# Sixteen attention weight tiles split early and kept in DRAM, and three smaller edits of an attention stage

## The chip, the cores and the metric

The kernel runs on one core of one Trainium2 chip. A core has five engines with queues of their own: TensorE (PE, matmuls), VectorE (DVE), ScalarE (ACT), GpSimd (POOL) and SyncE (SP, which issues the DMAs here). The metric is the device time of one execution, in microseconds, as the median of several; beside it stands one execution taken by the hardware profiler, and all rows below are of that one.

## The reference, cut to what matters

Two layers work on 512 tokens of width 1024, in float32. Each layer is a mixer and an MLP, and both end in `x = LN(alpha*x + (1+gate)*f(x*(1+scale)+shift))`, where shift, scale and gate are products of one conditioning vector with large "modulation" matrices. The mixer of the first layer is a gated linear attention, the one of the second is softmax attention over 64-token chunks, and the change is about the second:

```
q, k, v = split(u @ w_in + b_in, 3)              # 16 heads of 64
s = q*k / 8 + rel_bias[head, clipped distance]   # own chunk and the 8 before it
o = softmax(masked s) @ v
out = o @ w_out
mlp: square(relu(u @ w1)) @ w2                   # width 4096
```

A row of the softmax sums to one, so `softmax(s) @ (v + b)` is `softmax(s) @ v + b`.

## The kernel before, in words

Activations lie with the 1024 features on partitions, as eight tiles of 128 x 512. Every weight comes in units of 512 KB (128 x 1024, the eight 128 x 128 blocks that make one output tile). To get float32 accuracy from the faster float32r matmul, a unit is split on chip: `hi` is the unit rounded to float32r (a cast on ScalarE) and `lo = raw - hi` (a subtraction on VectorE, `lo_of`). A product is then three matmuls, hi*hi, hi*lo and lo*hi (`mm3`), so that one output tile (`mtile`) is 24 matmuls of 128 x 512. The activations are split in the same manner.

The list `plan` holds all units of the program in the order of their use. `emit_unit` takes the next one, issues its load on SyncE into a `raw` buffer (a pool of five) and its cast and subtraction, and puts the pair into the queue `ready_w`; `next_w` hands out one and `fill` keeps some units ahead. Pairs lie in the pool `wp` (four each of `whi` and `wlo`) or, for a few, in the pool `act` (26 tiles of 128 x 1024, `fhi` and `flo`, shared with all activations `ar` and `af`). Kinds of units: "w" as told, "p" with the subtraction on GpSimd, "e", "f" and "F" in `act` tiles, "a" a modulation unit: a load, and one VectorE operation that multiplies it with the conditioning vector and sums. The 48 modulation units that remain lie between the units of the first MLP, one after each of its 48 middle weights (`add_mlp`).

VectorE, ScalarE, GpSimd and TensorE run in the order of the program text, which the class `InOrder` fixes; every instruction recorded through it has line 46 of the kernel before (47 of the one after), so rows are told apart by the names of their tiles. The order of SyncE's queue is left to the scheduler of the framework. All engines wait for each other by semaphores, and a queue whose head waits holds back what is behind it.

Attention (`att`) begins with the value projections (`vpass`, two passes of four units) and goes on in a loop over six pairs of heads. An iteration makes one query tile and one key tile (`mtile` twice, evacuated by `evac_qk`, whose parts are `q_hi`, `q_lo`, `k_hi`, `k_lo`) and runs the softmax of two heads: `s_mm` the scores, `s_a` the evacuation with the bias and the maximum over keys, begun on VectorE and ended by an all-reduce on GpSimd (`mb`), `s_b1` the subtraction of the maximum on VectorE, `s_b2` the exponential on ScalarE, `pv` the product with the values, which also gives the sum of the row. A pair is divided by its sum in `fin1` (ScalarE: evacuation of the sum, and exp(-log) as a first reciprocal y), `fin2` (VectorE: one Newton step y(2 - sy) and the products) and `fin3` (split of the result). Six of the eight query and key pairs, p = 2 to 7, are projected in this loop; the first two come before it. The tail (`t1` to `t5`) finishes the last heads between the matmuls of the output projection `a_o`, whose first four units are kind "e".

Of the kernel before, what the change touches and what calls it, by code (L numbers as in the profile page):

```python
# [15 lines left out]
P = 128  # L16
# [39 lines left out]


@with_exitstack
def trunk(ctx, tc, xT, c, ada, cols, gk1, gk2, w_qk, w_v, w_g, w_go, a_qk, a_v, a_bv, a_tab,
          a_win, a_o, f1, f2, out):  # L60
    nc = tc.nc
    V, A, G, T = (InOrder(tc, e) for e in (nc.vector, nc.scalar, nc.gpsimd, nc.tensor))
# [4 lines left out]
    rawp = ctx.enter_context(tc.tile_pool(name="rawp", bufs=5))  # L67
    wp = ctx.enter_context(tc.tile_pool(name="wp", bufs=4))
    psp = ctx.enter_context(tc.tile_pool(name="psp", bufs=8, space=bass.MemoryType.PSUM))

    out_k = out.rearrange("(k p) s -> p k s", p=P)
    uid = [0]
# [52 lines left out]
    def ada_unit(l, t, k):  # L125
        raw = rawp.tile([P, D], F32, tag="raw", name=nm("raw"))
        nc.sync.dma_start(out=raw, in_=ada[l, t * 8 + k])
        if (l, t, k) == (0, SH1, 0):
            nc.sync.dma_start(out=col, in_=cols)
            for ll in range(2):  # L130
                for ty in (SC1, G1, SC2, G2):
                    b = C_ADA + ll * 48 + ty * 8
                    G.tensor_scalar(out=col[:, b:b + 8], in0=col[:, b:b + 8], scalar1=1.0, scalar2=None, op0=ALU.add)
            G.tensor_scalar(out=bq8, in0=col[:, C_BQ:C_BQ + 8], scalar1=0.125, scalar2=None, op0=ALU.mult)
            G.tensor_scalar(out=nbgk, in0=col[:, C_BGK:C_BGK + 4], scalar1=-1.0, scalar2=None, op0=ALU.mult)
            G.tensor_scalar(out=gn2, in0=col[:, C_GN:C_GN + 8], scalar1=-0.5, scalar2=None, op0=ALU.mult)
        if t == SC1 and l == 0:
            nc.sync.dma_start(out=xs[k], in_=xT[k * P:(k + 1) * P, :])
        i = t * 8 + k
        V.scalar_tensor_tensor(out=raw, in0=raw, scalar=1.0, in1=csil, op0=ALU.mult, op1=ALU.mult,  # L140
                               accum_out=mods[:, l, i:i + 1])
        if l == 0 and t in (SH1, SC1):
            if t == SC1:
                m2 = mods[:, 0, 0:16].rearrange("p (a b) -> p a b", b=8)[:, :, k:k + 1]
                c2 = col[:, C_ADA:C_ADA + 16].rearrange("p (a b) -> p a b", b=8)[:, :, k:k + 1]
                tt(V, m2, m2, c2, ALU.add)
        elif t == G2:
            tt(V, mods[:, l, i:i + 1], mods[:, l, i:i + 1], col[:, C_ADA + l * 48 + i:C_ADA + l * 48 + i + 1], ALU.add)
# [8 lines left out]
    state = {"pos": 0, "look": 0}  # L157
    ready_w, ready_f = [], []

    def emit_unit():  # L160
        kind, what = plan[state["pos"]]
        state["pos"] += 1
        if kind == "a":
            ada_unit(*what)
            return
        raw = rawp.tile([P, D], F32, tag="raw", name=nm("raw"))
        if state["pos"] == 3:
            for q in range(2):
                nc.sync.dma_start(out=raw[:, q * S:(q + 1) * S], in_=what[:, q * S:(q + 1) * S])
        else:  # L170
            nc.sync.dma_start(out=raw, in_=what)
        if kind in "eEfF":
            hi = act.tile([P, D], F32R, tag="act", name=nm("fhi"))
            lo = act.tile([P, D], F32R, tag="act", name=nm("flo"))
        else:
            hi = wp.tile([P, D], F32R, tag="whi", name=nm("whi"))
            lo = wp.tile([P, D], F32R, tag="wlo", name=nm("wlo"))
        if state["pos"] == 3:
            V.tensor_copy(hi[:, 0:S], raw[:, 0:S])
            later.append(lambda: A.copy(out=hi[:, S:D], in_=raw[:, S:D]))  # L180
            later.append(lambda: lo_of(V, lo, raw, hi))
            ready_w.append((hi, lo))
            return
        if kind == "s":
            for q in range(2):
                A.copy(out=hi[:, q * S:(q + 1) * S], in_=raw[:, q * S:(q + 1) * S])
        else:
            A.copy(out=hi, in_=raw)
        lo_of(G if kind in "pEF" else V, lo, raw, hi)
        (ready_f if kind in "fF" else ready_w).append((hi, lo))  # L190

    def fill(n=None):
# [28 lines left out]
    def add_out(units, fgs, adas=(), early=False, pool=0):  # L221
        adas = list(adas)
        for i, u in enumerate(units):
            plan.append(("e" if early and i < 4 else "p" if i < pool else "w", u))
            if fgs and not early and 1 < i < 6:
                plan.append(("f", fgs[i - 2]))
            if adas and i < 4:
                plan.append(("a", adas.pop(0)))
        for a in adas:
            plan.append(("a", a))  # L230
        if early:
            plan.extend(("fF"[i // 2], u) for i, u in enumerate(fgs))
# [10 lines left out]
    fg1 = lambda l: [f1[l, m] for m in range(4)]  # L243
    add_out([w_go[k] for k in range(8)], fg1(0))

    def add_mlp(l, fgs, ad):
        ad = list(ad)
        for m in range(4, 8):
            plan.append(("p" if m < 5 else "w", f1[l, m]))
        rest = [u for g in range(3) for u in [f2[l, g * 8 + m] for m in range(8)] + [f1[l, g * 8 + 8 + m] for m in range(8)]]  # L250
        add_units(rest, ad)
        add_out([f2[l, 24 + m] for m in range(8)], fgs)

    add_mlp(0, [a_qk[0], a_qk[8], a_qk[1], a_qk[9]], ada_list(0, G2) + ada_list(1, SH1, SC1, G1, SC2, SH2))
    add_units([a_v[k] for k in range(2)], kind="p")
    add_units([a_v[k] for k in range(2, 8)])
    for p in range(2, 8):
        add_units([a_qk[p], a_qk[8 + p]])
    add_out([a_o[k] for k in range(8)], fg1(1), early=True)
    add_mlp(1, [], ada_list(1, G2))  # L260

# [601 lines left out]
    def att(u):  # L863
# [37 lines left out]
        def s_a(h):  # L901
            sA, sB, b = sab[h]
            sAf = sA.rearrange("p a b -> p (a b)")
            s = [sAf[:, 0:S], sAf[:, S:S + 384], sB[:, 0, 0:256], sAf[:, S + 384:2 * S]]
            for j in range(4):
                ps = sps[h][j]
                off = max(W[j], 256) - W[j]
                nb = min(W[j], 256)
                stt(s[j][:, 0:nb], ps[:, off:off + nb], ng[:, h:h + 1], b[:, 0:nb], ALU.add, ALU.add)
                if W[j] > 256:  # L910
                    A.copy(out=s[j][:, 256:W[j]], in_=ps[:, 256:W[j]])
            mx = sB[:, 1, :]
            V.tensor_copy(mx[:, 0:P], s[0][:, 0:P])
            tt(V, mx[:, P:S], s[0][:, P:S], s[1], ALU.max)
            tt(V, mx[:, 256:S], mx[:, 256:S], s[2], ALU.max)
            tt(V, mx[:, 384:S], mx[:, 384:S], s[3], ALU.max)
            mb = ab_.tile([P, S], F32, tag="mb", name=nm("mb"))
            G.partition_all_reduce(mb, mx, P, bass_isa.ReduceOp.max)
            st[h] = (s, sAf)
            mbs[h] = mb  # L920
# [40 lines left out]
        def fin2(p):  # L961
            s, y, pa, pb = fin[p]
            tt(V, s, s, y, ALU.mult)
            V.tensor_scalar(out=s, in0=s, scalar1=-1.0, scalar2=2.0, op0=ALU.mult, op1=ALU.add)
            tt(V, y, y, s, ALU.mult)
            tt(V, s[0:64, :], pa[0:64, :], y[0:64, :], ALU.mult)
            tt(V, s[64:128, :], pb[64:128, :], y[64:128, :], ALU.mult)

        def fin3(p):
            s = fin[p][0]  # L970
            r = act_r()
            A.copy(out=r[:, 0, :], in_=s)
            lo_of(V, r[:, 1, :], s, r[:, 0, :])
            o.append(r)

        bv = act_f()
        nc.sync.dma_start(out=bv.rearrange("p a b -> p (a b)"), in_=a_bv.to_broadcast([P, D]))

        def vpass(n, hooks):
            pvb = [bank() for _ in range(4)]  # L980
            for j in range(4):
                w = next_w()
                for kk in range(2):
                    k = 2 * j + kk
                    for i in range(4):
                        mm3(pvb[i], uk(u, k, i * P, (i + 1) * P), wk(w, kk, S), k == 0, k == KT - 1)
                hooks[j]()
            for i in range(4):
                ov = vt[i][:, n * 4:(n + 1) * 4, :].rearrange("p a (b c) -> p a b c", c=64)[:, :, 0:3:2, :]
                tt(V, ov, pvb[i].rearrange("p (a b c) -> p a b c", b=2, c=64),  # L990
                   bv[:, n, :].rearrange("p (a b c) -> p a b c", b=2, c=64), ALU.add)

        def both(*fs):
            def f():
# [207 lines left out]
```

## Time and profile before

| | us |
|---|---|
| median of 3 runs | 1245.2 (1243.76 to 1246.84) |
| profiled execution | 1244.1 |
| its span | 1242.4, mean granted TensorE clock 0.984 |
| TensorE busy | 1189.6 (96%) |
| VectorE busy | 841.5 (68%) |
| ScalarE busy | 536.6 (43%) |
| GpSimd busy | 187.4 (15%) |
| DMA | 159.62 MB; HBM read 156.54, written 2.10 |

Busy shares are means over the whole span. The stages have different limits, so they are read one by one: the first MLP's long part lies at 300 to 557 us, attention begins at about 640, its loop at 689.7, its tail at 776.3, and the boundary to the second MLP at about 838. The view by windows gives the busy time of each engine in such a stretch, the chain of waits says which engine the end of the program hung on, and a timeline lists one engine's instructions in order; a bracket at a row's end is the idle time before it and what ended it. Rows of a timeline with a count join neighbours of one form.

### The profile page before, as it was taken

How to read it: one execution, taken by the hardware profiler on the slowest of the kernel's cores; microseconds unless marked ns; L12 is line 12 of the kernel's file. 1: busy time of each engine (PE TensorE's matmuls, PEld its weight loads, DVE VectorE, ACT ScalarE, POOL GpSimd, SP SyncE). 2: the span in 40 equal slices, each digit the busy share in tenths (PEclk: the TensorE clock that was granted, in tenths of full speed). 3: DMA queues.
4: the chain of work that ended last, by engine and by line, in shares of the span. 5: the costliest groups of instructions: out<-in, count | busy, mean ns of one | idle time of the engine just before them, and what ended most of it. 6: DMA issues, size and time to landing. Idle time of an engine off the chain costs nothing.

```text
span 1242.4 us, 15258 instructions
## 1 busy us (share of the span) xinstructions
PE 1189.6 (96%) x5834; PEld 992.7 (80%) x5834; DVE 841.5 (68%) x1297; ACT 536.6 (43%) x844; POOL 187.4 (15%) x195
## 2 busy tenths in 40 slices
PE   8999999899999999999899999889999999999995
PEld 5678888888888888888888776668888888888885
DVE  6679579786566565558855889999874443543467
ACT  3365565464232232342582656573651331422424
POOL 2000002620000000005531222226300000000035
PEclk9999999899999999999999999999999999999998
DMA  8746624126656556544042111222055233232201
GB/s 317 268 152 222 219 102 155 33 68 190 202 176 209 186 190 206 185 137 153 1 141 89 43 60 45 83 83 88 29 188 174 85 102 102 85 102 94 92 18 68
DMA packets 48200, 159.62 MB, mean 128 GB/s; under 512 B 5440, under 2 KB 9792, under 8 KB 48128
## 3 DMA queue, kind: packets, MB, share of 16 engines
q1 hardware_dynamic: 48128, 158.66, 38.5%
q8 instruction: 45, 0.74, 0.2%
q14 instruction: 27, 0.22, 0.1%
HBM read 156.54 MB, written 2.10 MB: 128 GB/s over the span
## 4 chain that ended last, share of the span: by engine, by line
PE 55%; DVE 21%; issue 9%; ACT 9%; POOL 3%; DMA 1%; ACTq 0%; DVEq 0%; SPq 0%; POOLq 0%
PE ps L46 55%; DVE af L46 7%; ACT af L46 3%; DVE x L46 3%; DVE ar L46 3%; DVE raw L46 2%; ACT ar L46 2%; DVE wlo L46 2%; ACT whi L46 2%; POOL af L46 1%; POOL x L46 1%; DVE u L46 1%; ACT e L46 1%; DVE d L46 1%; DMA raw<-w_v 1%
## 5 line engine op out<-in xcount | busy, mean ns | idle before, releaser
L46 PE MATMUL ps<-ar,whi 128*128 128x512 f32 (+1 forms) x2816 | 809.5, 375 | 6.5 <-ACT ar L46 3.5
L46 PEld LDWEIGHTS ps<-ar,whi 128*128 128x128 f32 x2816 | 517.3, 191 | 105.4 <-DVE ar L46 5.0
L46 PE MATMUL ps<-ar,wlo 128*128 128x512 f32 (+1 forms) x1408 | 515.0, 372 | 0.5 <-DVE wlo L46 0.4
L46 PEld LDWEIGHTS ps<-ar,wlo 128*128 128x128 f32 x1408 | 268.2, 190 | 47.5 <-DVE wlo L46 2.4
L46 ACT CAST whi<-raw 128x1024 fp32r<-128x1024 f32 (+1 forms) x183 | 184.0, 1013 | 241.6 <-PE ps L46 227.5
L46 DVE TENSOR_TENSOR wlo<-raw,whi 128x1024 fp32r<-128x1024 f32 x172 | 217.3, 1267 | 43.9 <-ACT whi L46 41.5
L46 DVE SCALAR_TENSOR_TENSOR x<-ps,mods,x 128x512 f32<-128x512 f32 (+1 forms) x96 | 63.1, 658 | 137.0 <-PE ps L46 137.0
L46 POOL TENSOR_TENSOR x<-x,af 128x512 f32<-128x512 f32 x14 | 24.7, 1794 | 807.5 <-ACT af L46 807.5
L46 DVE SCALAR_TENSOR_TENSOR raw<-raw,csil 128x1024 f32<-128x1024 f32 x96 | 115.8, 1218 | 5.9 <-DMA raw<-ada 5.9
L46 DVE TENSOR_TENSOR h<-r 128x512 f32<-128x512 f32 (+1 forms) x72 | 49.3, 689 | 92.1 <-ACT r L46 91.3
L46 PE MATMUL ps<-ar,fhi 128*128 128x256 f32 (+1 forms) x448 | 93.9, 307 | 8.6 <-DVE ar L46 7.6
L46 ACT ACTIVATE r<-ps 128x512 f32<-128x512 f32 (+1 forms) x72 | 39.1, 549 | 137.6 <-PE ps L46 137.3
L46 PEld LDWEIGHTS ps<-ar,fhi 128*128 128x128 f32 x448 | 73.4, 195 | 13.2 <-DVE ar L46 9.1
L46 PE MATMUL ps<-whi,ar 128*128 128x512 f32 x256 | 81.0, 391 | 0.4 <-ACT whi L46 0.4
L46 DVE TENSOR_TENSOR ar<-h,ar 128x512 fp32r<-128x512 f32 (+1 forms) x72 | 45.6, 633 | 39.5 <-ACT ar L46 38.4
L46 PE MATMUL ps<-ar,flo 128*128 128x256 f32 (+1 forms) x224 | 67.8, 303 | 0.0
L46 ACT CAST ar<-h 128x512 fp32r<-128x512 f32 (+1 forms) x72 | 41.2, 572 | 51.3 <-DVE h L46 51.3
L46 PEld LDWEIGHTS ps<-whi,ar 128*128 128x128 f32 x256 | 48.1, 188 | 11.2 <-ACT whi L46 1.3
L46 POOL PARTITION_ALL_REDUCE mb<-af x16 | 33.3, 2078 | 133.8 <-DVE af L46 133.8
L46 PE MATMUL ps<-wlo,ar 128*128 128x512 f32 x128 | 50.2, 392 | 1.5 <-DVE wlo L46 1.5
L46 ACT ACTIVATE af<-x 128x256 f32<-128x256 f32 (+1 forms) x48 | 22.7, 486 | 56.1 <-POOL af L46 31.5
L46 PEld LDWEIGHTS ps<-ar,flo 128*128 128x128 f32 x224 | 43.5, 194 | 1.5
(140 smaller groups left out, 1045.1 us busy)
## 6 DMA issues: line engine op xcount, KB each, us to landing
raw<-f SPq DMA_DIRECT2D x128, 512.0 KB, 3.5
raw<-ada SPq DMA_DIRECT2D x96, 512.0 KB, 4.6
raw<-a_qk SPq DMA_DIRECT2D x16, 512.0 KB, 3.6
raw<-w_v SPq DMA_DIRECT2D x8, 512.0 KB, 4.2
raw<-w_g SPq DMA_DIRECT2D x8, 512.0 KB, 4.4
raw<-w_go SPq DMA_DIRECT2D x8, 512.0 KB, 4.7
raw<-a_v SPq DMA_DIRECT2D x8, 512.0 KB, 3.6
raw<-a_o SPq DMA_DIRECT2D x8, 512.0 KB, 3.5
```

Source lines behind the costliest of these rows:

```text
L46: r = f(*a, **k)
```

## The change

Four things are edited.

1. Sixteen weight units of attention, the twelve query and key units of pairs 2 to 7 and the first four of the output projection, become kind "c" in the first MLP, one after every third weight there: a load, a cast into an `act` tile, a subtraction into another, and a store of each of the two to DRAM. In attention the kinds "x" (into `wp`) and "X" (into `act`) stand in their old places: two loads of 512 KB on SyncE, and nothing on ScalarE or VectorE.
2. The value bias is no longer loaded as a broadcast tile and added in `vpass`. There the eight evacuations are now four copies on VectorE and four on ScalarE; the bias is added to the divided heads in `fin3`.
3. `fin2` folds the step 2 - sy and the sign into three operations of the form (a op scalar) op b.
4. In `s_a` the first block of the maximum is copied by ScalarE.

```diff
         if kind == "a":
             ada_unit(*what)
             return
+        if kind in "xX":
+            hi, lo = split_w(kind == "X")
+            nc.sync.dma_start(out=hi.bitcast(F32), in_=kept[what][0])
+            nc.sync.dma_start(out=lo.bitcast(F32), in_=kept[what][1])
+            ready_w.append((hi, lo))
+            return
+        if kind == "c":
+            key, src = what
+            raw = rawp.tile([P, D], F32, tag="raw", name=nm("raw"))
+            nc.sync.dma_start(out=raw, in_=src)
+            hi, lo = split_w(True)
+            A.copy(out=hi, in_=raw)
+            lo_of(V, lo, raw, hi)
+            kept[key] = [dram.tile([P, D], F32, name=f"{n}_{key[0]}{key[1]}") for n in ("khi", "klo")]
+            nc.sync.dma_start(out=kept[key][0], in_=hi.bitcast(F32))
+            nc.sync.dma_start(out=kept[key][1], in_=lo.bitcast(F32))
+            return
...
-            plan.append(("e" if early and i < 4 else "p" if i < pool else "w", u))
+            plan.append(("X", ("o", i)) if early and i < 4 else ("p" if i < pool else "w", u))
...
+            if keep and i % 3 == 1:
+                plan.append(("c", keep.pop(0)))
...
-    for p in range(2, 8):
-        add_units([a_qk[p], a_qk[8 + p]])
+    for i in kqk:
+        plan.append(("x", ("q", i)))
...
-            V.tensor_copy(mx[:, 0:P], s[0][:, 0:P])
+            A.copy(out=mx[:, 0:P], in_=s[0][:, 0:P])
...
             tt(V, s, s, y, ALU.mult)
-            V.tensor_scalar(out=s, in0=s, scalar1=-1.0, scalar2=2.0, op0=ALU.mult, op1=ALU.add)
-            tt(V, y, y, s, ALU.mult)
-            tt(V, s[0:64, :], pa[0:64, :], y[0:64, :], ALU.mult)
-            tt(V, s[64:128, :], pb[64:128, :], y[64:128, :], ALU.mult)
+            stt(y, s, 2.0, y, ALU.subtract, ALU.mult)
+            stt(s[0:64, :], pa[0:64, :], -1.0, y[0:64, :], ALU.mult, ALU.mult)
+            stt(s[64:128, :], pb[64:128, :], -1.0, y[64:128, :], ALU.mult, ALU.mult)
...
-            A.copy(out=r[:, 0, :], in_=s)
-            lo_of(V, r[:, 1, :], s, r[:, 0, :])
+            bv = col[:, C_BV + p:C_BV + p + 1]
+            A.activation(out=r[:, 0, :], in_=s, func=AF.Identity, bias=bv)
+            stt(r[:, 1, :], s, bv, r[:, 0, :].bitcast(F32), ALU.add, ALU.subtract)
...
-                tt(V, ov, pvb[i].rearrange("p (a b c) -> p a b c", b=2, c=64),
-                   bv[:, n, :].rearrange("p (a b c) -> p a b c", b=2, c=64), ALU.add)
+                if i % 2:
+                    V.tensor_copy(ov, iv)
+                else:
+                    A.copy(out=ov, in_=iv)
```

VectorE in one iteration of the loop, from the key's low halves to the odd head's subtraction, before (`raw`, `whi` and `wlo` are a weight unit and its halves, the `af` of 128 x 512 with one name is the pair's sum and reciprocal, `mb` the maximum):

```order
L46 TENSOR_TENSOR ar_6030<-f_6028,ar_6030 64x512 x2
L46 TENSOR_TENSOR wlo_6054<-raw_6051,whi_6053 128x1024
L46 TENSOR_TENSOR af_6100<-af_6100 128x512
L46 TENSOR_SCALAR af_6100<-af_6100 128x512
L46 TENSOR_TENSOR af_6100<-af_6100 128x512
L46 TENSOR_TENSOR af_6100<-ps_6059,af_6100 64x512
L46 TENSOR_TENSOR af_6100<-ps_6064,af_6100 64x512
L46 TENSOR_TENSOR af_5929<-af_5929,mb_6041 128x512
```

The same place after:

```order
L47 TENSOR_TENSOR ar_6337<-f_6335,ar_6337 64x512 x2
L47 TENSOR_TENSOR af_6405<-af_6405 128x512
L47 SCALAR_TENSOR_TENSOR af_6405<-af_6405 128x512
L47 SCALAR_TENSOR_TENSOR af_6405<-ps_6364,af_6405 64x512
L47 SCALAR_TENSOR_TENSOR af_6405<-ps_6369,af_6405 64x512
L47 TENSOR_TENSOR af_6239<-af_6239,mb_6348 128x512
```

The split of a weight (`wlo`) and the constant step (`TENSOR_SCALAR`) are gone, and the three operations behind it have another form. Further on in the same iteration, from the even head's scores to the odd head's, before (`ps` is the scores, `ng` a bias column, `f` and `ar` the query tile and its halves):

```order
L46 SCALAR_TENSOR_TENSOR af_6094<-ps_6116,ng,af_6095 128x128
L46 COPY af_6095<-af_6094 128x128
L46 TENSOR_TENSOR af_6095<-af_6094 128x384
L46 TENSOR_TENSOR af_6095<-af_6095 128x256
L46 TENSOR_TENSOR af_6095<-af_6095,af_6094 128x128
L46 TENSOR_TENSOR wlo_6151<-raw_6148,whi_6150 128x1024
L46 TENSOR_TENSOR ar_6128<-f_6125,ar_6127 64x512 x2
L46 SCALAR_TENSOR_TENSOR af_6097<-ps_6185,ng,af_6098 128x256
```

And after:

```order
L47 SCALAR_TENSOR_TENSOR af_6399<-ps_6420,ng,af_6400 128x128
L47 TENSOR_TENSOR af_6400<-af_6399 128x384
L47 TENSOR_TENSOR af_6400<-af_6400 128x256
L47 TENSOR_TENSOR af_6400<-af_6400,af_6399 128x128
L47 TENSOR_TENSOR ar_6432<-f_6429,ar_6431 64x512 x2
L47 SCALAR_TENSOR_TENSOR af_6402<-ps_6487,ng,af_6403 128x256
```

The copy and the second split have left, so the query's low halves stand right behind the maximum. On ScalarE this place, from the even head's scores to the query's casts, was:

```order
L46 COPY af_6094<-ps_6114 128x256
L46 COPY af_6094<-ps_6115 128x128
L46 ACTIVATE af_5929<-af_5929 128x1024
L46 ACTIVATE af_5930<-af_5930 128x256
L46 CAST whi_6150<-raw_6148 128x1024
L46 CAST ar_6127<-f_6125 64x512 x4
L46 ACTIVATE f_6196<-ps_6160,col 128x512
L46 COPY af_6097<-ps_6185 128x256
```

and is now (`col` is the bias column):

```order
L47 ACTIVATE ar_6435<-af_6405,col 128x512
L47 COPY af_6399<-ps_6418 128x256
L47 COPY af_6399<-ps_6419 128x128
L47 COPY af_6400<-af_6399 128x128
L47 ACTIVATE af_6239<-af_6239 128x1024
L47 ACTIVATE af_6240<-af_6240 128x256
L47 CAST ar_6431<-f_6429 64x512 x4
L47 ACTIVATE f_6498<-ps_6462,col 128x512
```

The weight cast has left ScalarE's queue ahead of the query's casts, and the copy of the maximum stands ahead of the exponential. SyncE in the first MLP, before, one weight and one modulation unit in turn:

```order
L127 DMA raw_3547<-ada 128x1024
L171 DMA raw_3550<-f 128x1024
L127 DMA raw_3588<-ada 128x1024
L171 DMA raw_3591<-f 128x1024
L127 DMA raw_3629<-ada 128x1024
L171 DMA raw_3632<-f 128x1024
```

and after, over three such pairs (`khi` and `klo` are the DRAM tiles):

```order
L184 DMA raw_3776<-a_qk 128x1024
L197 DMA raw_3786<-f 128x1024
L129 DMA raw_3824<-ada 128x1024
L197 DMA raw_3827<-f 128x1024
L189 DMA khi_q_3782<-fhi_3778 128x1024
L129 DMA raw_3865<-ada 128x1024
L190 DMA klo_q_3783<-flo_3779 128x1024
L197 DMA raw_3868<-f 128x1024
L129 DMA raw_3906<-ada 128x1024
```

A load for the kept unit and two stores have come between; the second store stands right ahead of a weight load.

## Rows read from the trace of the kernel before

**Rows 1.** Busy time by stage: window, length, PE, PEld, DVE, ACT, POOL, PEclk, DMA, GB/s
```profile
300.00:557.00 257.00, 257.00 (x1135) 212.88 (x1134) 154.90 (x214) 78.30 (x98) 0.00 (x0) 1.00 0.57 188
689.70:776.30 86.60, 80.97 (x349) 61.89 (x348) 77.27 (x145) 55.13 (x93) 19.92 (x16) 0.98 0.17 53
776.30:838.60 62.30, 53.10 (x211) 40.01 (x210) 57.70 (x103) 40.02 (x64) 14.38 (x12) 0.93 0.25 82
```

**Rows 2.** Chain that ended last, window 640 to 900 us: start, length, what
```profile
641.68 47.96 PE ps L46 x217
...
837.38 2.52 PE ps L46 x5
```

**Rows 3.** VectorE timeline, one loop period: start, length, form, count, [idle before <-releaser]
```profile
711.35 1.53 DVE L46 SCALAR_TENSOR_TENSOR af<-ps,ng,af 128x256 f32<-128x256 f32 x4
...
712.79 0.22 DVE L46 COPY af<-af 128x128 f32<-128x128 f32 x1
...
714.18 2.54 DVE L46 TENSOR_TENSOR af<-af,mb 128x512 f32<-128x512 f32 x4
...
718.18 1.23 DVE L46 TENSOR_TENSOR wlo<-raw,whi 128x1024 fp32r<-128x1024 f32 x1
...
720.69 0.69 DVE L46 TENSOR_TENSOR af<-af 128x512 f32<-128x512 f32 x1 [1.28 <-ACT af L46]
...
721.41 0.43 DVE L46 TENSOR_SCALAR af<-af 128x512 f32<-128x512 f32 x1
...
724.11 1.70 DVE L46 TENSOR_TENSOR af<-af,mb 128x512 f32<-128x512 f32 x4
...
726.44 1.53 DVE L46 SCALAR_TENSOR_TENSOR af<-ps,ng,af 128x256 f32<-128x256 f32 x4
...
729.85 1.80 DVE L46 TENSOR_TENSOR wlo<-raw,whi 128x1024 fp32r<-128x1024 f32 x1 [0.49 <-ACT whi L46]
...
732.99 0.88 DVE L46 SCALAR_TENSOR_TENSOR af<-ps,ng,af 128x256 f32<-128x256 f32 x2
```

**Rows 4.** ScalarE timeline, the same period
```profile
716.75 1.36 ACT L46 ACTIVATE af<-af 128x1024 f32<-128x1024 f32 x2 [1.99 <-DVE af L46]
...
727.51 1.36 ACT L46 ACTIVATE af<-af 128x1024 f32<-128x1024 f32 x2
...
728.78 1.03 ACT L46 CAST whi<-raw 128x1024 fp32r<-128x1024 f32 x1
...
729.71 2.53 ACT L46 CAST ar<-f 64x512 fp32r<-64x512 f32 x4
```

**Rows 5.** GpSimd timeline, the same period
```profile
714.36 2.15 POOL L46 PARTITION_ALL_REDUCE mb<-af  x1 [4.69 <-DVE af L46]
...
729.52 1.79 POOL L46 PARTITION_ALL_REDUCE mb<-af  x1 [11.86 <-DVE af L46]
```

**Rows 6.** TensorE timeline, 755 to 780 us
```profile
760.87 1.60 PE L46 MATMUL ps<-ar,ar 128*128 128x512 f32 x8 [2.24 <-DVE ar L46]
762.26 1.06 PE L46 MATMUL ps<-ar,whi 128*128 128x512 f32 x2
```

**Rows 7.** Groups of instructions by form: busy us, mean ns, idle before
```profile
L46 ACT COPY af<-ps 128x128 f32<-128x128 f32 x16 | 4.3, 266 | 0.2
...
L46 ACT CAST gk_w<-gk_raw 128x128 fp32r<-128x128 f32 x1 | 0.3, 299 | 0.0
...
L46 DVE SCALAR_TENSOR_TENSOR af<-ps,gn,y 128x512 f32<-128x512 f32 x8 | 5.5, 743 | 0.1
```

**Rows 8.** Two windows of the program's start; then SyncE's waits, 300 to 557 us
```profile
0.00:50.00 50.00, 43.59 (x158) 30.50 (x159) 34.06 (x60) 16.23 (x24) 9.08 (x28) 0.97 0.89 315
...
5.00:16.00 11.00, 7.54 (x21) 4.78 (x20) 7.99 (x13) 3.66 (x4) 6.54 (x18) 0.84 1.01 399
...
SPq L171 <- DVE raw L46: 139.5, 35, 5.9
```

**Rows 9.** VectorE timeline, end of the attention tail
```profile
833.23 3.50 DVE L46 TENSOR_TENSOR wlo<-raw,whi 128x1024 fp32r<-128x1024 f32 x3
```

More of the change, by code (lines that the diff above doesn't have):

```diff
@@ L33 @@
 C_BK = 180
-N_COL = 188
+C_BV = 188
+N_COL = 196
 SH1, SC1, G1, SH2, SC2, G2 = range(6)
@@ L58, in trunk @@
 @with_exitstack
-def trunk(ctx, tc, xT, c, ada, cols, gk1, gk2, w_qk, w_v, w_g, w_go, a_qk, a_v, a_bv, a_tab,
+def trunk(ctx, tc, xT, c, ada, cols, gk1, gk2, w_qk, w_v, w_g, w_go, a_qk, a_v, a_tab,
           a_win, a_o, f1, f2, out):
@@ L69, in trunk @@
     psp = ctx.enter_context(tc.tile_pool(name="psp", bufs=8, space=bass.MemoryType.PSUM))
+    dram = ctx.enter_context(tc.tile_pool(name="dram", bufs=1, space=bass.MemoryType.DRAM))
     out_k = out.rearrange("(k p) s -> p k s", p=P)
@@ L158, in trunk, with split_w @@
     ready_w, ready_f = [], []
+    kept = {}
+    def split_w(in_act):
+        if in_act:
+            return (act.tile([P, D], F32R, tag="act", name=nm("fhi")), act.tile([P, D], F32R, tag="act", name=nm("flo")))
+        return (wp.tile([P, D], F32R, tag="whi", name=nm("whi")), wp.tile([P, D], F32R, tag="wlo", name=nm("wlo")))
     def emit_unit():
@@ L171, in emit_unit @@
             nc.sync.dma_start(out=raw, in_=what)
[L172 to L177, printed above, removed]
+        hi, lo = split_w(kind in "fF")
         if state["pos"] == 3:
@@ L188, in emit_unit @@
             A.copy(out=hi, in_=raw)
-        lo_of(G if kind in "pEF" else V, lo, raw, hi)
+        lo_of(G if kind in "pF" else V, lo, raw, hi)
         (ready_f if kind in "fF" else ready_w).append((hi, lo))
@@ L244, in trunk, with add_mlp @@
     add_out([w_go[k] for k in range(8)], fg1(0))
-    def add_mlp(l, fgs, ad):
+    def add_mlp(l, fgs, ad, keep=()):
         ad = list(ad)
@@ L250, in add_mlp @@
         rest = [u for g in range(3) for u in [f2[l, g * 8 + m] for m in range(8)] + [f1[l, g * 8 + 8 + m] for m in range(8)]]
-        add_units(rest, ad)
+        keep = list(keep)
+        for i, u in enumerate(rest):
+            plan.append(("w", u))
+            if ad:
+                plan.append(("a", ad.pop(0)))
+            if keep and i % 3 == 1:
+                plan.append(("c", keep.pop(0)))
+        assert not ad and not keep
         add_out([f2[l, 24 + m] for m in range(8)], fgs)
-    add_mlp(0, [a_qk[0], a_qk[8], a_qk[1], a_qk[9]], ada_list(0, G2) + ada_list(1, SH1, SC1, G1, SC2, SH2))
+    kqk = [q + p for p in range(2, 8) for q in (0, 8)]
+    add_mlp(0, [a_qk[0], a_qk[8], a_qk[1], a_qk[9]], ada_list(0, G2) + ada_list(1, SH1, SC1, G1, SC2, SH2),
+            [(("q", i), a_qk[i]) for i in kqk] + [(("o", i), a_o[i]) for i in range(4)])
     add_units([a_v[k] for k in range(2)], kind="p")
     add_units([a_v[k] for k in range(2, 8)])
-    for p in range(2, 8):
-        add_units([a_qk[p], a_qk[8 + p]])
+    for i in kqk:
+        plan.append(("x", ("q", i)))
     add_out([a_o[k] for k in range(8)], fg1(1), early=True)
@@ L971, in fin3 @@
             r = act_r()
-            A.copy(out=r[:, 0, :], in_=s)
-            lo_of(V, r[:, 1, :], s, r[:, 0, :])
+            bv = col[:, C_BV + p:C_BV + p + 1]
+            A.activation(out=r[:, 0, :], in_=s, func=AF.Identity, bias=bv)
+            stt(r[:, 1, :], s, bv, r[:, 0, :].bitcast(F32), ALU.add, ALU.subtract)
             o.append(r)
-        bv = act_f()
-        nc.sync.dma_start(out=bv.rearrange("p a b -> p (a b)"), in_=a_bv.to_broadcast([P, D]))
         def vpass(n, hooks):
@@ L989, in vpass @@
                 ov = vt[i][:, n * 4:(n + 1) * 4, :].rearrange("p a (b c) -> p a b c", c=64)[:, :, 0:3:2, :]
-                tt(V, ov, pvb[i].rearrange("p (a b c) -> p a b c", b=2, c=64),
-                   bv[:, n, :].rearrange("p (a b c) -> p a b c", b=2, c=64), ALU.add)
+                iv = pvb[i].rearrange("p (a b c) -> p a b c", b=2, c=64)
+                if i % 2:
+                    V.tensor_copy(ov, iv)
+                else:
+                    A.copy(out=ov, in_=iv)
         def both(*fs):
@@ L1177 @@
         "cols": np.concatenate([colsT(a["b_ada"]), colsT(a["ln_g"]), colsT(a["ln_b"]), colsT(a["gla_b_gk"]),
-                                colsT(a["gla_g_norm"]), colsT(a["att_b_in"][0, :2 * D])], axis=1),
+                                colsT(a["gla_g_norm"]), colsT(a["att_b_in"][0])], axis=1),
         "gk1": gw[:, 3072:].reshape(8, P, 16).transpose(1, 0, 2),
@@ L1186 @@
         "a_v": half(aw[:, 2 * D:]),
-        "a_bv": a["att_b_in"][:, 2 * D:],
         "a_tab": tab[:, 256][None, :],
```

## The prediction

> **What bounds the kernel now.** I read the busy time by stage first [rows 1]. In the first MLP (300 to 557 us) TensorE is busy 257.00 of 257.00 us at full clock, VectorE 154.90 and ScalarE 78.30: TensorE is the limit, and the rest hides behind it. In the head-pair loop of attention (689.7 to 776.3) it is busy 80.97 of 86.60, in the attention tail (776.3 to 838.6) 53.10 of 62.30, at a granted clock of 0.98 and 0.93.
>
> The chain of waits says the same [rows 2]: one TensorE piece of 47.96 us from 641.68, the value projections and what opens attention, then from 689.66 VectorE and ScalarE pieces in turn, until TensorE takes over again at 837.38. So attention from 689.66 to 838 is the one place here where less VectorE and ScalarE work can shorten the run. The loop is periodic: the scores of an odd head start at 711.35 and again at 732.99 [rows 3], 21.65 us apart, four such periods from 689.66 to 776.28.
>
> What TensorE could give back at most: its idle time, 86.60 - 80.97 + 62.30 - 53.10 = 14.8 us, and the lost clock, 0.02 x 86.6 + 0.07 x 62.3 = 6.1. After a gap of 2.24 us its pairs of matmuls take 1.06 us [rows 6]; that is the slow clock behind a wait. So about 20 us is the ceiling of any gain here.
>
> **The change part by part.** All sums are made against the profiled execution, 1244.1 us (span 1242.4); the median of the runs is 1245.2, and I add its 1.1 at the end.
>
> *Sixteen units move into the first MLP.* There they add 16 casts on ScalarE (1.03 us by the one in the loop [rows 4]), 16 subtractions on VectorE (1.23 [rows 3]), 16 loads and 32 stores of 512 KB. VectorE goes to 154.9 + 16 x 1.23 = 174.6 of 257 us, ScalarE to 94.8: both stay far below TensorE, whose matmuls don't change, so a gain is excluded. The DMA demand goes from 188 to about 188 + 48 x 0.524 MB / 257 us = 286 GB/s; worked from units (48 weights, 48 modulation units, 48 kept transfers, 75.5 MB) 294. The start of the program moved 315 GB/s on average over 50 us, and 399 over its best 11 [rows 8]. By those I take the cost as nothing; the work that hides it is TensorE's 257 us with weights split two tiles ahead. Where the cover goes: a store waits on SyncE for its ScalarE or VectorE half, and the next weight and modulation loads stand behind it in that queue. SyncE already waits 139.5 us in this stretch, in 35 waits for raw buffers that VectorE frees [rows 8]; the second store stands just ahead of such a load and waits for the same subtraction, so most of its wait replaces one that is there. Bounds: 0, or what a rate below the demand costs (third rival).
>
> The Trainium skill ("HBM Reference", Specifications) gives a core about 358 GB/s, half of its stack. By that figure the 75.5 MB would take 211 us, and the cost would be nothing too; the trace moved 399 for 11 us, so that figure is no ceiling for a core alone.
>
> *The value bias* leaves the evacuation of the value projections: eight VectorE additions become four copies there and four on ScalarE. All lie beside TensorE's unbroken 47.96 us [rows 2], so: nothing. It comes back in the last step of a pair, as a ScalarE instruction with a bias column in place of a cast, and a VectorE operation with a pointer scalar in place of a subtraction. The nearest row is 0.743, with a scalar from a column [rows 7], against 0.69 for the plain one [rows 3]: +0.05, and I take 0.06 with its rounding; at the other end nothing. The ScalarE one lies beside 1.70 us of VectorE work, the odd head's subtraction at 724.11 [rows 3].
>
> *The loop period.* I follow the cycle from the scores of the odd head (0) by VectorE's order. Scores, now without the copy, 2.83 - 0.13 = 2.70 (the copy is 0.22 long, but neighbours overlap by 0.09, as 711.35 + 1.53 against 712.79 shows [rows 3]). The subtraction of the maximum 2.54: 5.24. Here a removed split (the one at 718.18) buys nothing, since VectorE then waits 1.28 us for ScalarE at 720.69 [rows 3]; that wait grows to about 2.5. From ScalarE's exponential (716.75 [rows 4]) to 720.69 its exponentials, copies, logarithm and reciprocal take 3.94: 9.2. The refinement loses its constant step: 0.43 and its gap, 0.46 [rows 3]: the odd head's subtraction then starts at 12.1 in place of 12.76 (724.11 less 711.35). From there to the scores of the even head it was 2.33 (726.44 less 724.11 [rows 3]), now 2.39 with the dearer low half: 14.5. ScalarE's exponential began 1.07 after those (727.51 [rows 4]) and stands behind the evacuations in its queue; the new copy of the maximum goes between: 14.5 + 1.07 + 0.28 + 1.36 = 17.2. The price of that copy is not in the trace: 0.266 for this size from PSUM, 0.299 for a cast of this size in SBUF [rows 7]; I take 0.28, nearest to both, once per period on the path (at the odd head ScalarE waits 1.99 us for VectorE anyway [rows 4]). Then no weight cast (1.03 [rows 4]) stands before the four casts of the query (2.53 [rows 4]); the last subtraction on VectorE needs the third of them: 17.2 + 1.9 = 19.1, and with 0.69 the period ends at 19.8. Before, VectorE stood in a split of 1.80 us at that place [rows 3]. Gain: 21.65 - 19.8 = 1.85; I keep 0.1 for gaps that a handover brings, 1.75, times four periods: 7.0 us.
>
> One thing could eat of this. The split at 729.85 took 1.80 us against 1.23 at 718.18, and what ran beside it was the all-reduce on GpSimd (729.52, 1.79 us) [rows 3, 5]; the subtraction at 714.18, beside the all-reduce at 714.36, took 2.54, and 1.70 at 724.11 with none [rows 3, 5]. With the split gone, the query's low halves (2 x 0.69) move toward that all-reduce. It would run from 17.0 to 18.8, and only the first of them can touch it. Bounds: nothing, or 2 x 0.69 x (2.54 / 1.70 - 1) = 0.7 per period, 2.7 in all; I take nothing, as the second starts at 19.1.
>
> The Trainium skill ("SBUF — State Buffer", Who interferes with whom) says that a VectorE instruction with two SBUF inputs contends with a GpSimd one that reads SBUF. The rows just given agree with it. By that rule applied to both low halves the sum below would be 10.1 in place of 12.8.
>
> *The tail.* VectorE is busy 57.70 of its 62.30 us [rows 1], so nearly all that leaves it counts: four splits for the output projection, 1.23 each by the one at 718.18 [rows 3], 4.9; four constant steps at 0.43, 1.7; five copies at 0.13, 0.7; one split of the last key tile hidden before a wait. That is 7.3. Against it stand new waits for ScalarE, at the places where a split now covers it: I take 1.5, about one wait of the size at 720.69. Gain 5.8. The group of three splits that stands last before TensorE's restart (833.23, 3.50 us [rows 9]) stays. The two ends are 3 (each freed split turned into a wait) and 9.2, TensorE's idle time.
>
> *Loads in attention.* Sixteen units arrive as two loads each, on SyncE, and wait for the tile that TensorE left four units before, about 1.5 periods or 30 us ahead of use; the DMA share in the loop is 0.17 [rows 1]. Behind a load that waits stand the bias windows of the next heads and, after the last of them, the second MLP's first weights. I take nothing; if not, each late microsecond is one of TensorE's.
>
> Sum: 7.0 + 5.8 = 12.8; 1244.1 - 12.8 = 1231.3, and with the 1.1 of the median 1232.4.
>
> **The rivals.**
> 1. *TensorE becomes the limit again and its clock stays up.* For it: a period of TensorE alone is 21.65 less its share of the idle time (5.63 / 4 = 1.4) and of the lost clock (0.4), 19.8; the cycle above is just as long, and either may end last. If VectorE's waits overlap better than in my cycle and the gap of 2.24 us [rows 6] goes in loop and tail, the gain reaches the ceiling: 1245.2 - 20 = 1225. Against: by the cycle, ScalarE's exponentials and the query's casts are still in line.
> 2. *The gain turns into waits for ScalarE and GpSimd.* For it: VectorE already waits at 720.69 and 729.85 for ScalarE [rows 3], and the copy of the maximum is dearer on the engine that is next on the path. If the first wait grows by all that was freed and the low halves meet the all-reduce, the period gains 1.75 - 0.7 and the tail 3: about 7, 1238.
> 3. *Slower: the stores bind the first MLP.* Place: 300 to 557 us, SyncE's queue, where loads stand behind stores. The point from which it decides is a rate under 75.5 MB / (257 + 12.8) us = 280 GB/s for mixed loads and stores. At 250 GB/s the stretch takes 302 us, 45 longer: 1232.4 + 45 = 1277; at 270 it is 1255. For it: no row shows 512 KB stores, and 294 is the highest demand over 250 us in the program. Against: 315 over 50 us with a DMA share of 0.89 [rows 8].
> 4. *Nothing comes of it*: 1244 to 1247, if the loop's cycle is set by something I have not seen, such as a bank of PSUM that comes free late, or if about 13 us are lost in the first MLP.
>
> **How the numbers follow.** The forecast as worked out (1228 to 1236) has 0.52, rival 1 0.18, rival 2 0.14, rival 3 0.08, rival 4 0.08. The measurement tells 0.3% (3.7 us) from no change, so faster means under 1241.5: the forecast, rival 1 and rival 2 but for its edge, 0.83; same 0.09; slower 0.08. The range holds rival 1 and most of rival 2 and leaves out the slow side: 1222 to 1242. The likeliest one alone: 1228 to 1236.
>
> **What would show it.** Right: the first MLP stays at 257 us with TensorE at 257 and a DMA share near 0.86; the loop period falls to about 19.9 us, the wait at its fin2 grows to about 2.5, the tail shrinks to 55 to 56 us, and the chain still runs through VectorE and ScalarE there. Wrong: gaps on TensorE before 557, or waits for DMA of kept tiles; a period of 21 or more; a period near 18 with an unbroken TensorE piece in the chain (rival 1); the query's low halves at about 1.0 us (rival 2).

## The result and the profile after

The changed kernel takes 1233.6 us (median of 4 runs, 1231.7 to 1234.3) against 1245.25 for the kernel before: a ratio of 0.9904, 95% interval 0.9887 to 0.9921. Forecast were 1232.4, with a range of 1222 to 1242. The profiled execution's span is 1229.5 us, 12.9 less than before; the medians differ by 11.6, since the profiled execution of the changed kernel was the fastest of its four.

Where the 12.9 us came from is read off the chain of waits between 640 and 900 us (start, length, what):

```profile
641.10 95.05 PE ps L47 x427
736.14 0.59 ACT af L47
...
824.40 0.76 PE ps L47 x2
```

Against [rows 2], TensorE's first piece starts 0.58 us sooner, and it now reaches 95.05 us, far into the loop, in place of 47.96. TensorE takes over again at 824.40 in place of 837.38. From there to the end of the program nothing changes (1229.5 - 824.4 and 1242.4 - 837.4 are both 405). Split at the odd heads' scores: 0.5 us of the gain lie before the loop (689.66 to 689.12), 7.1 in its four periods, 5.3 in the tail. In the profiles of this study, that of the doubled stores left out, this piece starts anywhere between 641.0 and 642.0 without a pattern, so the 0.5 is not claimed for the change.

The same stretches by windows (window, length, busy PE, PEld, DVE, ACT, POOL, then PEclk, DMA share, GB/s):

```profile
300.00:557.00 257.00, 257.00 (x1135) 212.84 (x1134) 171.49 (x229) 92.88 (x113) 0.00 (x0) 1.00 0.80 280
689.12:768.62 79.50, 77.63 (x345) 60.57 (x344) 65.76 (x125) 48.68 (x93) 19.60 (x16) 1.00 0.31 110
768.62:824.40 55.78, 49.53 (x211) 37.01 (x209) 49.83 (x89) 36.63 (x64) 12.52 (x12) 1.00 0.31 100
```

Against [rows 1], the first MLP is as long as it was and TensorE as full, with VectorE up by 16.6 us, ScalarE by 14.6 and the DMA from 188 to 280 GB/s. In attention the granted clock reads 1.00 where it read 0.98 and 0.93.

One loop period on VectorE (start, length, form, count, idle before), to lay beside [rows 3]:

```profile
709.02 1.53 DVE L47 SCALAR_TENSOR_TENSOR af<-ps,ng,af 128x256 f32<-128x256 f32 x4
...
711.71 2.54 DVE L47 TENSOR_TENSOR af<-af,mb 128x512 f32<-128x512 f32 x4
...
718.22 0.69 DVE L47 TENSOR_TENSOR af<-af 128x512 f32<-128x512 f32 x1 [2.54 <-ACT af L47]
718.95 0.69 DVE L47 SCALAR_TENSOR_TENSOR af<-af 128x512 f32<-128x512 f32 x1
...
726.75 2.10 DVE L47 TENSOR_TENSOR ar<-f,ar 64x512 fp32r<-64x512 f32 x2 [0.40 <-ACT ar L47]
728.88 1.53 DVE L47 SCALAR_TENSOR_TENSOR af<-ps,ng,af 128x256 f32<-128x256 f32 x4
```

The period is 728.88 - 709.02 = 19.86, against 21.65 (19.88 as the mean of four, by the starts at 689.12 and 768.62). The wait at the pair's first product has grown from 1.28 to 2.54, the constant step behind it has gone, and before the next scores there is no weight's split, only the query's two low halves, with a wait of 0.40 for ScalarE's cast. ScalarE at that place, beside [rows 4]:

```profile
724.10 0.66 ACT L47 COPY af<-ps 128x256 f32<-128x256 f32 x2 [2.18 <-DVE af L47]
724.65 0.30 ACT L47 COPY af<-af 128x128 f32<-128x128 f32 x1
724.85 1.36 ACT L47 ACTIVATE af<-af 128x1024 f32<-128x1024 f32 x2
726.12 2.51 ACT L47 CAST ar<-f 64x512 fp32r<-64x512 f32 x4
```

The new copy of the maximum stands between evacuation and exponential; it takes 0.30 us, and the exponential begins 0.20 after it began. The casts of the query follow with no weight cast between.

### The profile page after: what moved, and what is told of

Read it like the earlier page. It is cut to its first block, busy times and chain, and to the rows that moved or that the text cites. A ratio compares the mean times of both kernels' runs of the same rounds, so it can differ in the third digit from the quotient of the medians.

```text
span 1229.5 us, 15417 instructions
## 1 busy us (share of the span) xinstructions
PE 1181.4 (96%) x5834; PEld 986.9 (80%) x5834; DVE 834.3 (68%) x1269; ACT 542.9 (44%) x864; POOL 185.4 (15%) x195
## 4 chain that ended last, share of the span: by engine, by line
PE 58%; DVE 20%; issue 9%; ACT 8%; POOL 3%; DMA 0%; ACTq 0%; DVEq 0%; POOLq 0%
PE ps L47 58%; DVE af L47 5%; ACT af L47 3%; DVE x L47 3%; DVE ar L47 3%; DVE raw L47 2%; DVE wlo L47 2%; ACT ar L47 2%; POOL af L47 1%; POOL x L47 1%; ACT whi L47 1%; DVE u L47 1%; DVE d L47 1%; DVE y L47 1%; ACT e L47 1%
## 5 line engine op out<-in xcount | busy, mean ns | idle before, releaser
L47 ACT CAST whi<-raw 128x1024 fp32r<-128x1024 f32 (+1 forms) x171 | 171.4, 1011 | 212.6 <-PE ps L47 187.0
L47 DVE TENSOR_TENSOR wlo<-raw,whi 128x1024 fp32r<-128x1024 f32 x160 | 199.9, 1254 | 33.3 <-ACT whi L47 31.2
L47 PEld LDWEIGHTS ps<-ar,fhi 128*128 128x128 f32 x448 | 71.9, 191 | 12.6 <-DVE ar L47 9.0
L47 ACT CAST ar<-h 128x512 fp32r<-128x512 f32 (+1 forms) x72 | 41.2, 573 | 51.8 <-DVE h L47 51.8
```

Of the source, the lines that this page charges most:

```text
L47: r = f(*a, **k)
```

## The experiments

Two theories were tried against each other all through. The first, the prediction's, says that the loop is a closed cycle through VectorE and ScalarE, so that what leaves this cycle is gained and what it covers is not. The rival says that with 95 us of TensorE in one piece, TensorE itself sets the loop now. Ratios below are to the kernel before, with their 95% intervals.

**The sixteen units alone.** Edits 2 to 4 undone (the diff is cut):

```diff
-            A.copy(out=mx[:, 0:P], in_=s[0][:, 0:P])
+            V.tensor_copy(mx[:, 0:P], s[0][:, 0:P])
...
-            stt(y, s, 2.0, y, ALU.subtract, ALU.mult)
+            V.tensor_scalar(out=s, in0=s, scalar1=-1.0, scalar2=2.0, op0=ALU.mult, op1=ALU.add)
+            tt(V, y, y, s, ALU.mult)
```

(and the value bias as before).

> The sixteen kept units alone; the value bias, the refinement and the copy of the maximum are as in the kernel before. Theory (a closed cycle through VectorE and ScalarE sets the loop at 19.88 us, and what leaves that cycle is gained): the constant step comes back (+0.46 per period), the copy on VectorE at the odd head (+0.13), the dearer low half and the copy on ScalarE go (-0.06, -0.20): a period of 20.2 us, the tail 57.5 in place of 55.8; together about 9.5 us faster than before, 1235.7. Rival (the small edits carry most of the gain): a period above 21 and under 4 us gained, above 1241. Rival (TensorE sets the period now): the period stays at 19.9 although the constant step is back.

Measured: 1236.0 us, ratio 0.9929 (0.9913 to 0.9946); period 20.25, tail 57.7. With the three edits undone the period is 0.37 longer, where their terms above add to 0.33, so TensorE did not set it. The run does not tell the three edits apart.

**The small edits alone**, with all weights split where they were (an empty list of kept units, kinds "w" and "e" in attention).

> The three small edits alone; all weights are split where they were. Theory: per period 0.46 less for the constant step, 0.13 less for the copy at the odd head, 0.06 more for the low half, 0.20 more on ScalarE at the even head: 21.65 - 0.33 = 21.3 us; the tail 61.1 - 1.7; about 3 us faster than before, 1242.2. The rest of the 11.6 is then the units'. Rival (small edits carry): 1236 or less.

Measured: 1240.6, ratio 0.9962 (0.9949 to 0.9975); tail 59.2 as expected, but a period of 21.01 in place of 21.3. The even head's scores and the second split on VectorE help to see why; the all-reduce beside the split stands at 728.02 on GpSimd, 1.78 us long:

```profile
725.05 1.53 DVE L47 SCALAR_TENSOR_TENSOR af<-ps,ng,af 128x256 f32<-128x256 f32 x4
...
728.65 1.49 DVE L47 TENSOR_TENSOR wlo<-raw,whi 128x1024 fp32r<-128x1024 f32 x1 [0.82 <-ACT whi L47]
```

The split takes 1.49 us here and took 1.80 [rows 3]. Counted from the scores, the all-reduce starts 0.11 us sooner than before, as the copy is gone from VectorE, and the split 0.19 later, as the copy now stands before its cast on ScalarE. So 1.15 us of the all-reduce lie beside the split in place of 1.46 [rows 3, 5]. That saving exists only while the split is there, which is part of why the two halves (9.4 and 4.8 us) add to more than the whole, 11.6.

**Twelve units**, those of the output projection split in the tail again.

> As changed, but the four units of the output projection are loaded raw and split in the tail as before; twelve are kept. Theory: the loop period stays at 19.88; the tail takes back four splits of 1.23 us, less 1.0 that they cover of waits for ScalarE, about 4 us: 1237.6. Rival (TensorE is near its limit in the tail and the splits were covered there): the tail stays within 1 us of 55.8, 1234.

Measured: 1237.2, ratio 0.9933 (0.9919 to 0.9948); period 19.88, tail 59.3, that is 3.5 more. So the query and key units made the loop's gain and the four output units 3.5 of the tail's 5.3.

**The copy of the maximum on VectorE again** (the first two lines of the diff above).

> As changed, but the first copy of the maximum is on VectorE again. Theory: 0.20 us less before the exponential at the even head, 0.13 more on VectorE at the odd head: a period of 19.8, and the tail within 0.5 us; the time within 1.5 us of the changed kernel's 1233.6. Rival (the copy's move was a gain): the period rises by 0.13 or more, and the tail by 5 x 0.13: 1235 or more. Rival (the move was a loss): 19.6, 1232.

Measured: 1233.95, ratio 0.9908 (0.9893 to 0.9923); period 19.85, tail 56.3. Moving the copy gains nothing and loses nothing that these runs tell apart: what it takes off VectorE at the odd head it puts on ScalarE at the even one. The run also shows how to read the chain. TensorE's first piece is 47.95 us here and 95.05 in the changed kernel, at the same period and nearly the same time:

```profile
641.90 47.95 PE ps L47 x217
```

Where the changed kernel's chain leaves TensorE (736.14), ScalarE had no idle time, so two paths end there almost together. A long piece of one engine in the chain is no proof that this engine sets the period.

**Every store twice**, to see how much room the first MLP has left:

```diff
             nc.sync.dma_start(out=kept[key][0], in_=hi.bitcast(F32))
+            nc.sync.dma_start(out=twin[0], in_=hi.bitcast(F32))
             nc.sync.dma_start(out=kept[key][1], in_=lo.bitcast(F32))
+            nc.sync.dma_start(out=twin[1], in_=lo.bitcast(F32))
```

> As changed, but each of the 32 stores in the first MLP is made twice, the second time to a DRAM tile that nobody reads. The changed kernel moved 280 GB/s there at a DMA share of 0.80, so a full share would be 350; with the second stores the demand is 92.3 MB in 257 us, 359 GB/s. Theory (the first MLP has room for what was added, and not for twice that): the stretch grows by some 7 us, TensorE shows gaps there, about 1240. Rival (stores cost no DMA time that loads need): 257 us stay, 1234. Rival (loads behind stores in SyncE's queue are already close to late): far more than 7 us, above 1250.

Measured: 1236.3, ratio 0.9921 (0.9903 to 0.9939), 2.7 us more than the changed kernel, where the theory said about 6 and the first rival none. The window of the first MLP, then what ScalarE waited for in it (engine, line, waited for: us in all, times, longest):

```profile
300.00:557.00 257.00, 255.90 (x1126) 210.91 (x1125) 171.38 (x231) 91.80 (x111) 0.00 (x0) 1.00 0.93 345
```

```profile
ACT whi L47 <- DMA raw<-f: 93.6, 27, 9.2
```

In the changed kernel the same casts waited mostly for TensorE:

```profile
ACT whi L47 <- PE ps L47: 75.1, 23, 4.4
...
ACT whi L47 <- DMA raw<-f: 4.7, 1, 4.7
```

At 345 GB/s many casts wait for their loads, yet TensorE loses only 1.1 us of this window. Mixed loads and stores therefore moved at least 345 GB/s, well above the 280 that the third rival needed. That is no ceiling: the window carried 71.9 MB in the changed kernel and 88.6 here, all the second stores of its units on top. The rest of the 2.7 us lies behind the window; TensorE's long piece at attention begins at 643.74.

**No all-reduce**: the maximum over keys is left out and zero is subtracted.

```diff
-            G.partition_all_reduce(mb, mx, P, bass_isa.ReduceOp.max)
+            G.memset(mb, 0.0)
```

> As changed, but the all-reduce of the maximum on GpSimd is left out and a constant zero is subtracted (a memset of 128x512 on GpSimd stands in its place). Theory (the loop is a cycle through VectorE and ScalarE, and TensorE, whose own period is 17.8 us, waits): the even head's subtraction takes 1.70 in place of 2.54, the query's first low half 0.69 in place of 1.30, which hides behind a cast; the period falls from 19.88 to 19.0, the tail by 2 to 3 us: 1227.5. Rival (TensorE sets the loop): period 19.9, 1233. Rival (the 2.54 is not contention with the all-reduce): it stays 2.54, and so does the period.

Measured: 1225.3, ratio 0.9837 (0.9822 to 0.9853); period 18.89, 0.99 less, and the tail 51.8, 4.0 less where 2 to 3 were expected. On VectorE, the query's two low halves and the even head's subtraction:

```profile
705.94 0.68 DVE L47 TENSOR_TENSOR ar<-f,ar 64x512 fp32r<-64x512 f32 x1 [0.40 <-ACT ar L47]
707.21 0.69 DVE L47 TENSOR_TENSOR ar<-f,ar 64x512 fp32r<-64x512 f32 x1 [0.59 <-ACT ar L47]
...
710.63 1.69 DVE L47 TENSOR_TENSOR af<-af,mb 128x512 f32<-128x512 f32 x4
```

The subtraction takes 1.69 where it took 2.54, and the first low half 0.68. Both were stretched by the all-reduce beside them, and the loop followed: TensorE had room. Of the 0.99 the subtraction makes 0.85; the low halves make the other 0.14, since the second starts 1.27 us after the first here and 1.41 in the changed kernel.

**Twenty and twenty-four kept units**, with all eight of the output projection, and then also the second MLP's first four (the diff shows only how the units are spread over the first MLP):

```diff
-            if keep and i % 3 == 1:
+            if keep and i % 12 in (1, 3, 6, 8, 11):     # twenty; i % 2 == 1 for twenty-four
```

> As changed, with all eight units of the output projection kept, twenty units in place of sixteen (five after every twelve weights of the first MLP). Demand there 81.8 MB in 257 us, 318 GB/s, a share of 0.91 by the changed kernel's ratio. Theory: the first MLP stays at 257; of the tail's four splits the three at its very end (3.50 us) leave the path and the first one was covered by a wait: 3.3 us less, 1230.3. Rival (loads arrive late): TensorE waits for the new tiles or in the first MLP, 1233 or more.

Measured: 1231.45, ratio 0.9886 (0.9870 to 0.9901), 2.2 us less than the changed kernel.

> As changed, with all eight units of the output projection and the first four weights of the second MLP kept, twenty-four units, one after every second weight of the first MLP. Demand 88.1 MB in 257 us, 343 GB/s, a share of 0.98 by the changed kernel's ratio. Theory: at the edge; if the loads hold, the tail gives the 3.3 us of twenty units and the two splits on VectorE behind it (4.24 us beside GpSimd's) some 3 more: 1227. Rival (the DMA binds in the first MLP): TensorE waits there, and the sum is no better than with twenty units, 1230 or more.

Measured: 1229.1, ratio 0.9868 (0.9851 to 0.9886). The first MLP kept its 257 us with TensorE full, at 305 and 330 GB/s. Of the 3.3 us expected of the last splits about 2 came. With twenty units the chain shows why, beside VectorE's end of the tail:

```profile
811.71 12.00 PE ps L47 x50
```

```profile
817.64 0.69 DVE L47 TENSOR_TENSOR af<-af 128x512 f32<-128x512 f32 x1 [1.79 <-ACT af L47]
...
821.37 0.75 DVE L47 SCALAR_TENSOR_TENSOR ar<-af,col,ar 128x512 fp32r<-128x512 f32 x1 [0.79 <-ACT ar L47]
823.74 1.43 DVE L47 SCALAR_TENSOR_TENSOR x<-ps,mods,x 128x512 f32<-128x512 f32 x2 [1.62 <-PE ps L47]
```

Waits for ScalarE now stand where splits were, but the end of the tail no longer hangs on them: TensorE works without a gap from 811.71 to 823.71, and VectorE waits 1.62 us for it. The tail's end is at TensorE's limit. With twenty-four units this piece is 17.78 us long, and another 2.4 us of the time went.

**The even head's subtraction and exponential ahead of the odd head's scores**, on the changed kernel and then with twenty-four units:

```diff
+                s_b1(2 * p + 2)
+                s_b2(2 * p + 2)
                 s_a(2 * p + 3)
                 k_hi()
-                s_b1(2 * p + 2)
                 k_lo()
                 fill(2)
-                s_b2(2 * p + 2)
```

> As changed, with one thing in another order in the loop: the even head's subtraction and exponential come before the odd head's scores on VectorE and ScalarE, where they came after. Nothing is added or removed. Theory (a closed cycle through VectorE and ScalarE sets 19.88 us, TensorE's own period is 17.8): the subtraction runs clear of the all-reduce, 1.70 in place of 2.54, and ScalarE's exponential starts at 1.7 in place of 5.24 of the cycle; followed by the same order as in the prediction the period comes to 18.2, and the loop to 6.6 us less: 1227. Rival (TensorE or the all-reduce sets the loop): 19.9, 1233.6. Rival (the odd head's scores, now later, keep their PSUM banks and delay TensorE): above 1234.

Measured: 1228.1, ratio 0.9855 (0.9841 to 0.9868), 5.5 less where 6.6 were expected; period 18.16 but for the first, which takes 19.42. VectorE, the chain, and TensorE's scores of the odd heads:

```profile
707.20 1.70 DVE L47 TENSOR_TENSOR af<-af,mb 128x512 f32<-128x512 f32 x4
708.82 1.52 DVE L47 SCALAR_TENSOR_TENSOR af<-ps,ng,af 128x256 f32<-128x256 f32 x4
...
726.99 1.52 DVE L47 SCALAR_TENSOR_TENSOR af<-ps,ng,af 128x256 f32<-128x256 f32 x4
```

```profile
641.23 136.53 PE ps L47 x615
```

```profile
706.36 1.44 PE L47 MATMUL ps<-ar,ar 128*128 128x512 f32 x8
...
724.16 1.45 PE L47 MATMUL ps<-ar,ar 128*128 128x512 f32 x8
```

The subtraction runs clear of the all-reduce, and the period is 1.7 us shorter, by nothing but an order. The all-reduce now lies beside the key's low halves, which take 2.13 us for the two in place of 1.40. TensorE works without a wait through the whole loop, and the tail begins when it is done. Its own period is still 17.80, shorter than VectorE's 18.17, so the cycle through VectorE and ScalarE remains the slower of the two; but it loses only some 0.35 us a period, and the loop ends before TensorE has to wait for it. For this loop as a whole TensorE is now the limit.

> Twenty-four kept units and the other order together. Theory: the two work at different places, the loop and the tail with the boundary, so they add: 1229.1 less 6.6, 1222.5. Rival (with the loop shorter, loads of kept tiles come late, at 1.8 us less per period): waits of TensorE for DMA, 1225 or more.

Measured: 1224.2, ratio 0.9825 (0.9812 to 0.9839), the fastest kernel here that leaves nothing out: 21.4 us less than before, with a period of 18.16 and no wait of TensorE for a DMA, so the rival's reason did not come. The two gains nearly add: 4.5 and 5.5 of the changed kernel's time by themselves, 9.4 together.

## Why the prediction was right

The sum was 7.0 for the loop, 5.8 for the tail, nothing elsewhere; the trace has 7.1, 5.3 and 0.5 of scatter. The mechanism held too: the loop followed the cycle through VectorE and ScalarE. Some terms were off by amounts that partly cancel. By its steps:

- *First MLP: nothing.* Right. TensorE stayed at 257.00 of 257.00. The share came to 0.80 where about 0.86 was named, at 280 GB/s. SyncE's waits changed as described; the longest sums in that stretch are now

```profile
SPq L129 <- DVE raw L47: 56.7, 20, 5.8
SPq L189 <- ACT fhi L47: 36.0, 13, 4.9
...
SPq L190 <- DVE flo L47: 12.5, 15, 1.0
```

  The store of the first half (L189) waits 36.0 us for its cast, and the store of the second (L190), which stands just ahead of a load with the same wait, 12.5; no load behind them came late for TensorE. The third rival needed a rate under 280 GB/s; the run with the doubled stores moved 345.
- *Value bias: nothing in the projections, 0.06 a pair in the last step.* Right; that operation takes 0.746 us on average against 0.69. No run undoes this edit alone.
- *Loop period 19.8 plus 0.05 kept for handovers.* Measured 19.88. The first removed split bought only a longer wait (2.54, named as about 2.5), the constant step and the weight cast were gained, and the copy of the maximum cost ScalarE 0.20 from start to start where 0.28 was taken. Its net is nothing, by the run that undoes it.
- *The low halves beside the all-reduce: no cost.* Nearly right, for the reason given: it was 0.14 us a period, against a bound of 0.7. The first was stretched to 1.30, as the chain of waits of the changed kernel shows at the third period:

```profile
746.08 0.52 ACT ar L47
746.62 1.30 DVE ar L47
...
748.03 0.69 DVE ar L47
```

  but the second begins at 748.03, 0.11 after it. In the run without the all-reduce the first takes 0.68 and VectorE then waits 0.59 for the third cast of the query; so most of the stretch lies where VectorE would have waited, and the rest is the 0.14. The Trainium skill ("SBUF — State Buffer", Who interferes with whom) says that a VectorE instruction with two SBUF inputs contends with a GpSimd one that reads SBUF, and not with one that only writes it. The runs agree. Beside the all-reduce the times are 2.54 and 1.30, without it 1.69 and 0.68; and beside a memset, which only writes, the key's low halves in the changed kernel keep their 1.40 for the two:

```profile
711.96 2.08 POOL L47 PARTITION_ALL_REDUCE mb<-af  x1 [3.49 <-DVE af L47]
714.10 1.09 POOL L47 MEMSET ar<- 64x512 f32 x2
```

```profile
714.28 1.40 DVE L47 TENSOR_TENSOR ar<-f,ar 64x512 fp32r<-64x512 f32 x2
```

  The even head's subtraction, 0.85 us a period dearer beside the all-reduce, was so in the kernel before as well; the new order frees it.
- *Tail 55 to 56 us.* Measured 55.78. The sum was 7.3 off VectorE less 1.5 of new waits. VectorE's busy time fell by 7.9 (57.70 [rows 1] to 49.83), and its waits for ScalarE there by the view of waits rose by 2.7 (from 1.8 to 4.5, three waits each). Both terms were taken too small, and the errors partly cancel: the good agreement here is in part luck.
- *TensorE's own period of 19.8 us, in the first rival: wrong.* It was had by taking a quarter of the window's idle time, and the lost clock, off the loop's period. TensorE's score matmuls of the odd heads in the changed kernel stand at

```profile
706.27 1.45 PE L47 MATMUL ps<-ar,ar 128*128 128x512 f32 x8
...
724.08 1.44 PE L47 MATMUL ps<-ar,ar 128*128 128x512 f32 x8
```

  17.81 us apart with no wait between. In the kernel before they stand at 689.00, 706.81 and 724.65, and only then at 746.22 and 769.30. VectorE takes up the first of these at 689.66, 0.7 us behind TensorE, and the third at 732.99 [rows 3], 8.3 behind: TensorE runs ahead at its own pace for two periods before it has to wait. So the loop's window holds more than four of its periods, and a quarter of the window's busy time is too long for one. The forecast did not rest on this figure, but the rival's chance did: the changed loop was not at TensorE's limit, 2 us a period were still to be had, and the new order took 1.7 of them. One named sign, a chain through VectorE and ScalarE, came only in part: the chain stays on TensorE to 736.14. The run with the copy back on VectorE shows that this says nothing of the period.

The second rival (a gain of 7) failed, since the low halves cost 0.14 a period in place of 0.7 and the tail used most of the time that was freed. The fourth, that nothing would come of it, failed with the measured 11.6 us.

## What to carry to other kernels

Follow the order of one engine around one loop period, with the waits, and ask of each removed instruction whether a wait stands right behind it: the split before the 1.28 us wait only made that wait longer (2.54), and the period's gain from the units, 1.1 us beside the small edits (21.01 to 19.88), must have come from the other split and its cast. Work that does not depend on a stage's data, here the split of a weight, can be moved to a stage that another engine bounds, if its DMA has room; here 92 GB/s more for 257 us were free. And look at the order before taking work away: one exchange of two steps in the loop was worth 5.5 us, more than half of what all the moved splits gave by themselves (9.4).

## What the runs showed of the hardware

- A waiting TensorE does not always lose its clock. Before, 2.24 us of idle time were followed by pairs of matmuls at 1.06 us [rows 6], at a granted clock of 0.71 over the next 3.1 us. After the changed kernel's wait of 1.12 us they run on at full rate:

```profile
754.84 1.53 PE L47 MATMUL ps<-ar,ar 128*128 128x512 f32 x8 [1.12 <-DVE ar L47]
756.21 0.63 PE L47 MATMUL ps<-ar,whi 128*128 128x512 f32 x2
```

  That is 0.63 us for a pair, and the granted clock is 1.00 in that window. But the length of one wait does not decide it. One period earlier the kernel before waited nearly as long, and ran on at the full 2.4 GHz:

```profile
739.22 1.53 PE L46 MATMUL ps<-ar,ar 128*128 128x512 f32 x8 [2.20 <-DVE ar L46]
740.59 0.62 PE L46 MATMUL ps<-ar,whi 128*128 128x512 f32 x2
```

  And a wait of 1.89 us, at 782.42, was followed by a granted clock of 0.53 over the next 3.6 us. In the tail the clock went from 0.93 to 1.00 as waits became fewer and shorter; no run changes the waits alone, so that this is the cause is not shown.
- Loads and stores of 512 KB together moved 345 GB/s over 257 us, at a DMA share of 0.93. ScalarE's casts then waited 93.6 us in all for loads, and TensorE lost 1.1 us. At 330 GB/s, with twenty-four units, TensorE lost nothing in this window.
- A partition all-reduce on GpSimd stretched VectorE operations with two SBUF inputs beside it: 1.69 to 2.54 us for the four parts of the even head's subtraction, 0.68 to 1.30 for 64x512; a memset beside such an operation did not (1.40 for two of 64x512).
